# Summing squares on VectorE in fp32 ahead of the ones-matmul of every norm

## The chip, the cores and the metric

The kernel runs on all 8 cores of one Trainium2 chip. Each core has one sequence of the batch and the cores exchange nothing. The metric is the device time in microseconds (us) of the slowest core. A program on 8 cores has a second, slower state in some of its executions: the cores of one die, or of both, show a lower granted TensorE clock, and the run is longer. Only fast runs are compared here, unless a sentence says otherwise.

The notes on the chip that this document draws on are called the Trainium skill; its pages are named by their titles.

## The reference, cut to what matters

A decoder block: a SwiGLU feed-forward (FFN1), a token mixer (a convolution branch beside a linear recurrence), a second SwiGLU feed-forward (FFN2), a final norm. Sequence 4096, width 1024, hidden width 2816. Every stage starts with a root-mean-square norm, and the convolution branch has a layer norm over 512 channels.

```python
def rmsnorm(x, g):
    xf = x.astype(jnp.float32)
    y = xf * lax.rsqrt(jnp.mean(xf * xf, axis=-1, keepdims=True) + EPS)
    return y.astype(x.dtype) * g

def layernorm(x, g, b):
    xf = x.astype(jnp.float32)
    mu = jnp.mean(xf, axis=-1, keepdims=True)
    var = jnp.mean(jnp.square(xf - mu), axis=-1, keepdims=True)
    ...

def swiglu_ffn(h, w_in, w_out):
    gate, up = jnp.split(h @ w_in, 2, axis=-1)
    return (jax.nn.silu(gate) * up) @ w_out
```

## The kernel before

Channels lie on partitions and tokens on the free axis. A tile is 512 tokens; its 1024 channels are 8 chunks of 128 x 512 in fp32. So a mean over channels is a sum over the 8 chunks and over the 128 partitions. The kernel does both on TensorE: each chunk is squared into a bf16 buffer, and a matmul with a 128 x 128 matrix of ones, accumulated in PSUM over the chunks, leaves the total on every partition.

```python
def stats(xs, after=(), prio=None):
    bank = new(ps, "st")
    for f in range(8):
        q = new(p1, "xsq")                        # a bf16 buffer
        o, i = (lambda q=q: q.ap), (lambda f=f: xs[f].ap)
        act(o, i, AF.Square, [xs[f]], [q], after=after, prio=prio, alt=v_sq(o, i))
        mms(bank, [(k_(ones.ap), lambda q=q: q.ap)], [q, ones], first=(f == 0), last=(f == 7), prio=prio)
    r = new(p2, "r")                              # then 1/sqrt as exp(-0.5 ln(.)) on ScalarE
    ...
```

`alt` lets a list scheduler put the square on VectorE instead of ScalarE. There are four such statistics per tile (FFN1, mixer, FFN2, final), so 32 of 8 ones-matmuls. The layer norm sums 4 chunks and their squares, 8 ones-matmuls in each of 8 tiles:

```python
bm, bq = new(ps, "lm"), new(ps, "lq")
for c in range(4):
    b, q = new(p1, "cvb"), new(p1, "cvsq")
    cp(lambda b=b: b.ap, lambda c=c: cv[c].ap, [cv[c]], [b])      # cast to bf16 on VectorE
    act(o, i, AF.Square, [cv[c]], [q], alt=v_sq(o, i))
    mms(bm, [(k_(ones.ap), lambda b=b: b.ap)], [b, ones], first=(c == 0), last=(c == 3))
    mms(bq, [(k_(ones.ap), lambda q=q: q.ap)], [q, ones], first=(c == 0), last=(c == 3))
```

That is 32 x 8 + 8 x 8 = 320 ones-matmuls.

The scheduler orders every instruction of the program ahead of time. Among the operations that can start now on an engine it takes the lowest `prio`, else the one that can start first, with planned durations. Each engine, the DMA-issuing ones (SP, POOL) included, then works through its own list in order, with semaphore waits:

```python
now = s <= et[e] + 0.03
key = (0 if now else 1, op.prio + (sw and 0.5) if now else s + sw, op.idx)
```

Three more places matter. FFN1 runs first for all tiles, in pairs, with `prio` 500 to 800, and stores its result x to DRAM ("xmid"). Then mixer, FFN2 and final norm run tile by tile, and read xmid back:

```python
def mix_ffn2(t):
    P.prio = 1000 + 10 * t
    gate_op = (last_in, anchors[-1][1])[t] if t < 2 else ffn_anchor[t - 2]
    xs = load_x(xm_dr, t, after=(gate_op,) * 8)     # 8 loads of 256 KB, issued by SP
    hb = norm(xs, M_SC2, M_SH2, prio=940)           # the mixer norm
```

Weights come in "slabs" of 128 x 2048 bf16 through ten slab buffers. On first use a slab is cast on its way in by a POOL DMA, and written back to DRAM in bf16 by SP for later tiles. Most weights of the second phase are cast during FFN1 (`prep`), but not those of FFN2's down-projection, "w2o", whose 12 slabs are cast on first use, in tile 0:

```python
def load_slab(nm, r, cast, prio=None, after=()):
    b = new(sl, f"{nm}{r}")
    if cast:
        dma("PL", lambda: b.ap, lambda: src, D_CAST, ..., [], [b], slab=True, ...)   # fp32 -> bf16
        dma("SP", lambda: d.ap, lambda: b.ap, D_SLAB, ..., [b], [d], prio=prio)      # write back
    else:
        dma("SP", lambda: b.ap, lambda: d.ap, D_SLAB, slot_sem(b), [d], [b], slab=True, ...)
...
prep = [(nm, r) for nm in ("win", "dcw", "wout", "w2i") for r in range(len(scr[nm]))]
...
slabs = [load_slab("w2o", 3 * q + s, t == 0) for s in range(3)]
```

## Time and profile before

| | before |
|---|---|
| device time, 3 fast runs | 2488.01, 2489.81, 2493.35 us |
| spans of the cores in the profiled run | 2468.5 to 2483.8 us, granted clock 0.991 to 0.993 |
| ones-matmuls | 320 |
| one more matmul in a dense row | 0.216 us |
| one fp32 128x512 VectorE add | 0.683 us |

The page of the slowest core, core 6: span, busy time by engine, TensorE's busy tenths in 40 slices of the span, and the shares of the chain that ended last (followed back from the last instruction, at each step to what released it). PEld is TensorE's loading of weights; a q after a name is the queue that waits and issues for that engine.

```profile
span 2483.8 us, 34258 instructions; the slowest of 8 cores (2468.5 to 2483.8 us)
PE 2361.1 (95%) x11177; PEld 1114.5 (45%) x11392; DVE 1057.8 (43%) x1795; ACT 911.9 (37%) x1382; POOL 115.2 (5%) x221
PE   1999999999999999899899999999999999999996
PE 90%; DMA 5%; ACT 2%; issue 1%; SPq 1%; DVE 1%; POOL 0%; DVEq 0%; POOLq 0%; ACTq 0%
```

TensorE (PE) is the bound: 95% busy, 90% of the chain. The four slices that aren't 9 are where it stands still: the start (weights arrive by DMA), slices 17 and 20 (the first mixer norm, and a stop near 1230 us) and the tail. VectorE (DVE) has more than half of its time free.

Groups of instructions of the same core, shapes kept apart. The columns after the count are busy us and mean ns of one; then the idle time of the engine before them and what ended most of it.

```profile
L443 PE MATMUL ps<-sb_h,sb_ones 128*128 128x512 bf16 x313 | 106.6, 394 | 67.0 <-ACT sb_h L401 59.6 <-DVE sb_h L413 6.5
L443 PEld LDWEIGHTS ps<-sb_h,sb_ones 128*128 128x128 bf16 x320 | 31.2, 98 | 118.5 <-issue 92.6
L423 DVE TENSOR_TENSOR sb_c<-sb_c 128x512 f32<-128x512 f32 x96 | 61.6, 683 | 11.1 <-ACT sb_c L401 11.0
L433 DVE CAST sb_h<-sb_c 128x512 bf16<-128x512 f32 x64 | 25.9, 420 | 0.6
```

The trace has lost 7 of the 320 ones-matmuls, but none of their weight loads, so weight loads are what to count by. A mean of 394 ns isn't what one costs: matmuls are pipelined, and their ends are modelled. The cost is read from starts. The timeline of PE in the steady part, core 6, columns start, us, instruction:

```profile
1334.16 0.38 PE L443 MATMUL ps<-sb_h,sb_ones 128*128 128x512 bf16 x1
1334.37 1.89 PE L443 MATMUL ps<-sb_h,sb_slab 128*128 128x512 bf16 x8
1336.10 0.38 PE L443 MATMUL ps<-sb_h,sb_ones 128*128 128x512 bf16 x1
```

The ones-matmul starts at 1334.16 and the next matmul at 1334.37: 0.21 us, no more than between any two of the eight that follow (1336.10 - 1334.37 = 1.73 us for 8). So 224 ones-matmuls are worth at most 224 x 0.216 = 48 us.

The stop near 1230 us is the second place to know. PE on core 6, then the issue queue of SP, then the chain of waits over the same stretch:

```profile
1214.70 12.47 PE L443 MATMUL ps<-sb_h,sb_slab 128*128 128x512 bf16 x56
1236.60 0.58 PE L443 MATMUL ps<-sb_h,sb_ones 128*128 128x512 bf16 x1 [9.43 <-ACT sb_h L401]
1236.98 6.18 PE L443 MATMUL ps<-sb_h,sb_slab 128*128 128x512 bf16 x16
```

```profile
1193.31 29.86 SPq L450 DMA_DIRECT2D b_w2o<-sb_slab  x7
1223.37 4.96 SPq L450 DMA_DIRECT2D sb_c<-xmid  x8
```

```profile
1207.86 14.94 DMA sb_slab<-w2o
...
1223.37 12.38 DMA sb_c<-xmid
...
1235.83 0.64 ACT sb_h L401
```

PE stands 9.43 us before the ones-matmul at 1236.60. The profile names ScalarE (ACT), but its square took 0.64 us: the chain shows that it waited for an xmid load, issued at 1223.37 and landed 12.38 us later, and that SP could issue it only after a writeback that itself waited for a cast of w2o, which took 14.94 us from issue to landing. The stop costs a second time. The windows view gives the busy time of PE, PEld, DVE, ACT and POOL in a stretch, the granted clock, the DMA share and GB/s:

```profile
1227.00:1237.00 10.00, 0.57 (x3) 0.23 (x3) 1.44 (x2) 1.15 (x2) 0.00 (x0) 0.75 1.05 251
1237.00:1243.00 6.00, 6.00 (x18) 2.17 (x17) 0.00 (x0) 3.15 (x5) 0.00 (x0) 0.57 0.97 305
1500.00:1680.00 180.00, 178.14 (x875) 86.55 (x890) 91.31 (x159) 89.53 (x134) 4.31 (x8) 1.00 0.55 182
```

The Trainium skill, "TensorE: Matmul & The Clock Gate", section "What's actually happening", says that an idle window of about 3.4 us halves the clock and a busy one of that length restores it. The trace agrees: the granted clock after the stop is 0.57, and 16 matmuls take 6.18 us where a warm row would take 15 x 0.216 + 0.38 = 3.62. In the single records the first thirteen start 0.43 us apart and the last three 0.21 to 0.25: the full rate is back about 5.5 us after the stop ends. The DMA engines are full at 1.05 during the stop. The last line is the steady part: PE busy 178.14 of 180 us, VectorE 91.31.

### The profile page before, as it was taken

What the parts mean: (1) busy time and instruction counts of PE and PEld (TensorE: products, weight loads), DVE (VectorE), ACT (ScalarE), POOL (GpSimd) and SP (SyncE); (2) the same over time, 40 slices, a digit from 0 to 9 for tenths busy, and PEclk for the clock granted to TensorE, in tenths of its full rate; (3) what the DMA queues carried; (4) which work ended last, traced back from release to release, by engine and by line L of the source; (5) the groups of instructions that cost most, each with busy time, mean ns of one, the idle gap of its engine ahead of it and who ended that gap; (6) DMA issues with size and microseconds to landing.
All of it is one profiled execution on the core that took longest, in us unless ns stands there. A gap on an engine that the chain in (4) does not pass through costs nothing.

```text
span 2483.8 us, 34258 instructions; the slowest of 8 cores (2468.5 to 2483.8 us)
## 1 busy us (share of the span) xinstructions
PE 2361.1 (95%) x11177; PEld 1114.5 (45%) x11392; DVE 1057.8 (43%) x1795; ACT 911.9 (37%) x1382; POOL 115.2 (5%) x221
## 2 busy tenths in 40 slices
PE   1999999999999999899899999999999999999996
PEld 0444444444444444454354454454454454454442
DVE  3413133423342332785166175184274274373121
ACT  3213011301131120676157265265364364364122
POOL 0100100010001001000000000000000000000000
PEclk9999999999999999899999999999999999999998
DMA  9899489669856764554966555555555545555451
GB/s 274 192 217 230 160 213 221 165 189 220 221 166 181 188 189 164 163 166 159 200 207 203 186 179 178 187 178 179 187 178 178 187 170 187 187 170 186 153 188 66
DMA packets 131708, 460.31 MB, mean 185 GB/s; under 512 B 16048, under 2 KB 16176, under 8 KB 130864
## 3 DMA queue, kind: packets, MB, share of 16 engines
q1 hardware_dynamic: 113184, 378.15, 47.0%
q0 software_dynamic: 18352, 79.97, 16.0%
q8 instruction: 96, 1.57, 0.3%
q14 instruction: 76, 0.62, 0.1%
HBM read 446.78 MB, written 79.69 MB: 212 GB/s over the span
## 4 chain that ended last, share of the span: by engine, by line
PE 90%; DMA 5%; ACT 2%; issue 1%; SPq 1%; DVE 1%; POOL 0%; DVEq 0%; POOLq 0%; ACTq 0%
PE ps L443 90%; DMA sb_slab<-wmod 2%; DMA sb_c<-x 1%; SPq L450 1%; DMA sb_c<-xmid 1%; ACT sb_c L401 1%; DMA sb_slab<-w2o 1%; ACT sb_h L401 1%; DVE sb_c L419 0%; DVE sb_c L409 0%; DVE sb_slab L499 0%; DVE sb_ub L419 0%; ACT L401 0%; POOL y L450 0%; DVEq L113 0%
## 5 line engine op out<-in xcount | busy, mean ns | idle before, releaser
L443 PE MATMUL ps<-sb_h,sb_slab 128*128 128x512 bf16 x9776 | 2182.2, 380 | 28.7 <-ACT sb_h L401 15.8
L443 PEld LDWEIGHTS ps<-sb_h,sb_slab 128*128 128x128 bf16 x9984 | 977.7, 98 | 1196.1 <-issue 30.4
L423 DVE TENSOR_TENSOR sb_h<-ps,sb_c 128x512 bf16<-128x512 f32 x352 | 241.7, 691 | 784.0 <-PE ps L443 706.5
L401 ACT ACTIVATE sb_c<-ps 128x512 f32<-128x512 f32 x400 | 237.2, 596 | 882.0 <-PE ps L443 858.5
L401 ACT ACTIVATE sb_h<-sb_c 128x512 bf16<-128x512 f32 x241 | 148.9, 628 | 387.2 <-DVE sb_c L419 234.4
L419 DVE SCALAR_TENSOR_TENSOR sb_c<-ps,sb_gth,sb_c 128x512 f32<-128x512 f32 x128 | 95.2, 749 | 399.1 <-PE ps L443 390.6
L401 ACT ACT_TABLE_LOAD x102 | 130.9, 1283 | 211.5 <-PE ps L443 199.2
L419 DVE SCALAR_TENSOR_TENSOR sb_c<-sb_c,sb_gs 128x512 f32<-128x512 f32 x256 | 173.6, 745 | 39.9 <-ACT sb_c L401 39.9
L443 PE MATMUL ps<-sb_h,sb_ones 128*128 128x512 bf16 x313 | 106.6, 394 | 67.0 <-ACT sb_h L401 59.6
L499 DVE SCALAR_TENSOR_TENSOR sb_slab<-sb_slab,sb_crow 128x1024 f32<-128x1024 f32 x88 | 107.0, 1217 | 34.1 <-DMA sb_slab<-wmod 33.6
L443 PE MATMUL ps<-sb_ub,sb_slab 128*128 128x256 bf16 x1024 | 115.0, 273 | 4.3 <-DVE sb_c L409 3.3
L401 ACT ACTIVATE sb_h<-sb_c,sb_modv 128x512 bf16<-128x512 f32 x162 | 107.4, 719 | 15.6 <-DVE sb_modv L423 8.8
L443 PEld LDWEIGHTS ps<-sb_ub,sb_slab 128*128 128x128 bf16 x1024 | 99.5, 98 | 21.5 <-issue 8.1
L450 POOL DMA_DIRECT2D y<-sb_c x64 | 34.5, 540 | 1144.6 <-ACT sb_c L401 1104.7
L443 PEld LDWEIGHTS ps<-sb_h,sb_ones 128*128 128x128 bf16 x320 | 31.2, 98 | 118.5 <-issue 92.6
L419 DVE SCALAR_TENSOR_TENSOR sb_c<-ps,sb_modv,sb_c 128x512 f32<-128x512 f32 x64 | 48.0, 750 | 72.7 <-PE ps L443 72.5
L419 DVE SCALAR_TENSOR_TENSOR sb_c<-sb_ux,sb_vecs,sb_c 128x512 f32<-128x512 f32 x96 | 69.2, 743 | 1.3
L423 DVE TENSOR_TENSOR sb_c<-sb_c 128x512 f32<-128x512 f32 x96 | 61.6, 683 | 11.1 <-ACT sb_c L401 11.0
L419 DVE SCALAR_TENSOR_TENSOR sb_ub<-sb_c,ps 64x256 bf16<-64x256 f32 x128 | 53.8, 420 | 15.3 <-PE ps L443 11.8
L401 ACT ACTIVATE sb_c<-sb_c,sb_lam 128x512 f32<-128x512 f32 x64 | 49.1, 824 | 0.2
L450 POOL DMA_DIRECT2D xmid<-sb_c x64 | 34.8, 544 | 295.6 <-DVE sb_c L419 280.6
L401 ACT ACTIVATE sb_c<-sb_c 128x512 f32<-128x512 f32 x72 | 44.0, 626 | 2.2
(51 smaller groups left out, 532.8 us busy)
## 6 DMA issues: line engine op xcount, KB each, us to landing
sb_slab<-b_w2i SPq DMA_DIRECT2D x176, 512.0 KB, 3.8
sb_slab<-wmod SPq DMA_DIRECT2D x88, 512.0 KB, 6.1
sb_slab<-b_w2o SPq DMA_DIRECT2D x84, 512.0 KB, 3.7
sb_slab<-b_w1i SPq DMA_DIRECT2D x66, 512.0 KB, 6.0
sb_slab<-b_win SPq DMA_DIRECT2D x64, 512.0 KB, 4.0
sb_slab<-b_dcw SPq DMA_DIRECT2D x64, 512.0 KB, 3.6
sb_slab<-b_w1o SPq DMA_DIRECT2D x36, 512.0 KB, 5.5
sb_c<-x SPq DMA_DIRECT2D x64, 256.0 KB, 11.0
```

The lines of the kernel that those rows point to most:

```text
L401: return A("ACT", dur, lambda: (lambda o, i: (lambda h: [h.activation(out=o, in_=i, func=func, bias=bias, scale=scale)]))(out(), in_()), r ...
L419: return A("DVE", dur, lambda: (lambda o, a, b: (lambda h: [h.scalar_tensor_tensor(out=o, in0=a, scalar=scalar, in1=b, op0=op0, op1=op1)]) ...
L423: return A("DVE", dur, lambda: (lambda o, a, b: (lambda h: [h.tensor_tensor(out=o, in0=a, in1=b, op=op)]))(out(), in0(), in1()), reads, wr ...
L443: return [h.matmul(o, lhsT=l, rhs=r, start=(first and i == 0), stop=(last and i == n - 1)) for i, (l, r) in enumerate(pr)]
L450: lambda: (lambda o, i: (lambda h: [h.dma_start(out=o, in_=i)]))(out(), in_()),
L499: return lambda h: [h.scalar_tensor_tensor(out=w, in0=w, scalar=1.0, in1=crow.ap, op0=ALU.mult, op1=ALU.mult, accum_out=o)]
```

## The change

The intent: add the fp32 squares of four chunks on VectorE, which has time, and give TensorE the sum, so that a statistic needs 2 ones-matmuls instead of 8. In the layer norm, chunks and squares are added in pairs: 4 ones-matmuls instead of 8, and the pair add writes bf16, so it replaces two casts. The squares move from bf16 to fp32 buffers. The first hunk, which only gives the helper `tt` a `prio` argument, is cut.

```diff
# (the hunk of the helper tt is cut)
@@ -532,11 +532,19 @@
         def stats(xs, after=(), prio=None):
 
             bank = new(ps, "st")
-            for f in range(8):
-                q = new(p1, "xsq")
-                o, i = (lambda q=q: q.ap), (lambda f=f: xs[f].ap)
-                act(o, i, AF.Square, [xs[f]], [q], after=after, prio=prio, alt=v_sq(o, i))
-                mms(bank, [(k_(ones.ap), lambda q=q: q.ap)], [q, ones], first=(f == 0), last=(f == 7), prio=prio)
+            for hf in range(2):
+                acc, sm = None, None
+                for f in range(4 * hf, 4 * hf + 4):
+                    q = new(p2, "xsq")
+                    o, i = (lambda q=q: q.ap), (lambda f=f: xs[f].ap)
+                    act(o, i, AF.Square, [xs[f]], [q], after=after, prio=prio, alt=v_sq(o, i))
+                    if acc is None:
+                        acc = q
+                        continue
+                    d = acc if f % 4 < 3 else new(p1, "sqb")
+                    tt(lambda d=d: d.ap, lambda q=q: q.ap, lambda acc=acc: acc.ap, ALU.add, [q, acc], [d], prio=prio)
+                    acc = d
+                mms(bank, [(k_(ones.ap), lambda d=acc: d.ap)], [acc, ones], first=(hf == 0), last=(hf == 1), prio=prio)
             r = new(p2, "r")
             act(lambda: r.ap, lambda: bank.ap, AF.Ln, [bank, cst], [r], bias=eps_ap, scale=1.0 / D, tset=(NLE,), prio=prio)
             act(lambda: r.ap, lambda: r.ap, AF.Exp, [r], [r], scale=-0.5, tset=(NLE,), prio=prio)
@@ -745,13 +753,20 @@
             A("DVE", 0.25, lambda: (lambda h: [h.tensor_copy(out=ub_t[:, :, 0:15], in_=ub_t[:, :, 256:271])]), [], ub)
 
             bm, bq = new(ps, "lm"), new(ps, "lq")
-            for c in range(4):
-                b, q = new(p1, "cvb"), new(p1, "cvsq")
-                cp(lambda b=b: b.ap, lambda c=c: cv[c].ap, [cv[c]], [b])
-                o, i = (lambda q=q: q.ap), (lambda c=c: cv[c].ap)
-                act(o, i, AF.Square, [cv[c]], [q], alt=v_sq(o, i))
-                mms(bm, [(k_(ones.ap), lambda b=b: b.ap)], [b, ones], first=(c == 0), last=(c == 3))
-                mms(bq, [(k_(ones.ap), lambda q=q: q.ap)], [q, ones], first=(c == 0), last=(c == 3))
+            for c in range(2):
+                a, e = cv[2 * c], cv[2 * c + 1]
+                b = new(p1, "cvb")
+                tt(lambda b=b: b.ap, lambda a=a: a.ap, lambda e=e: e.ap, ALU.add, [a, e], [b])
+                sq = []
+                for v in (a, e):
+                    q = new(p2, "cvsq")
+                    o, i = (lambda q=q: q.ap), (lambda v=v: v.ap)
+                    act(o, i, AF.Square, [v], [q], alt=v_sq(o, i))
+                    sq.append(q)
+                q = new(p1, "cvsb")
+                tt(lambda q=q: q.ap, lambda s=sq[0]: s.ap, lambda s=sq[1]: s.ap, ALU.add, sq, [q])
+                mms(bm, [(k_(ones.ap), lambda b=b: b.ap)], [b, ones], first=(c == 0), last=(c == 1))
+                mms(bq, [(k_(ones.ap), lambda q=q: q.ap)], [q, ones], first=(c == 0), last=(c == 1))
             mean, var = new(p2, "mean"), new(p2, "var")
             act(lambda: mean.ap, lambda bm=bm: bm.ap, AF.Copy, [bm], [mean], scale=1.0 / 512)
             act(lambda: var.ap, lambda bm=bm: bm.ap, AF.Square, [bm], [var], scale=1.0 / 512)
```

> **What bounds the kernel.** TensorE. The page gives PE 2361 of 2484 us busy (95%); the chain of waits is 90% PE; VectorE is at 43%, ScalarE at 37%. Matmuls start every 0.216 us (chain pieces of 10.74 us hold 49). The Trainium skill, "TensorE: Matmul & The Clock Gate", section "Wait — 56ns, not 53.3ns?", has 215.7 ns for a warm 512-column bf16 matmul; the trace agrees. In 180 us of the steady part PE is busy 178.3 (windows view). PE stands still in four places: before 65.8 us (weights by DMA), 5 us before 232 (a late x chunk ahead of a ones-matmul), about 11 us in 1000-1012 (first mixer norm), 9.4 us before 1236.6 (late xmid).
>
> **Removed.** 32 root-mean-square statistics go from 8 ones-matmuls to 2, and 8 layer norms from 8 to 4: 320 ones-matmuls become 96, 224 fewer. A lone one pushes the next matmul back by 0.22 us in the timeline (1334.16 to 1334.37), so weight switching adds nothing. At most 224 x 0.216 = 48 us (1.9%).
>
> **What does not count.** 12 of the first pair run while PE waits for weights; 12 of the second pair stand in the wait that ends at 232; 12 of the first mixer norms in the stop at 1000-1012; the last tile's 6 in the wait for the last square. Left: 182 x 0.216 = 39 us.
>
> **Added.** 192 fp32 adds, and 32 pair adds for 32 casts, on VectorE: 192 x 0.69 + 32 x (0.69 - 0.42) = about 141 us, to about 1200 us (49%). That two-input fp32 form lasts 0.683 us in the trace. The Trainium skill, "VectorE: DVE Perf Modes", section on mode 2x_2P, says fp32 tensor_tensor stays at 1x; the trace agrees, beside 0.42 for the one-input cast. Per steady tile that is 18 adds, 12.4 us, on 91.5 of 180 us. VectorE is 80-98% busy for only some 40 us around the recurrence and the convolution's evictions; there I expect 0.4 us more PE waiting per tile, about 3 us. Each statistic ends one add later (0.8 us), bare only in the tail and at one or two stage starts: 1.5 us. The squares move to the 40-buffer fp32 pool; the order listing shows later x loads displaced by only one or two places, so I charge nothing.
>
> **Reordering.** In the PE order the second pair's ones-matmuls now come after 16 to 28 more weight matmuls, and at the mixer's start two instead of sixteen precede the first projection matmuls. The stops at 227-232 and 1000-1012 may shrink by 0-4 us each: about 3 us together.
>
> **Sum.** 2490 - 39 - 3 + 3 + 1.5 = about 2452 us, 1.5% faster; range 2443 to 2463. Faster by over 2% (under 2440) needs nearly all 48 us or a stop to vanish: 7%. Within 2%: 92%. Slower: 1%.
>
> **What would show it.** Ones-matmuls x96; PE busy down 45-50 us by the page; the steady tile's period down from 179.5 to about 175 us; 240-990 shorter by about 5 us (24 fewer matmuls); VectorE near 1200 us; the tail 0.8 us longer; PE's waits for VectorE adds a few us in all.
>
> **What would make it wrong.** An add waiting for a late x or xmid chunk, in VectorE's in-order queue ahead of SwiGLU products or evictions, stalls PE (a longer stop at 220-236 or 1227-1240); more PE waiting in the mixer from VectorE; the fp32 pool running short and delaying loads; the stops at stage starts shifting by more than 4 us.

## The result, and the profile after

| | before | after |
|---|---|---|
| fast runs of the same rounds | 2488.01, 2489.81, 2493.35 us | 2449.68, 2452.52, 2454.54 us |
| slow runs | 2537.59 us | 2525.91 us (one die at clock 0.957 to 0.969) |
| ratio of fast runs, 95% interval | | 0.9847 (0.9823 to 0.987) |

Ratios are computed as the mean time of one kernel's fast runs over that of the other's in the same rounds, so not quite the ratio of the medians. The change makes the kernel 1.5% faster, within 2%. The median of its fast runs, 2452.52 us, is 0.5 us from the predicted 2452; over all four runs, the slow one included, it is 2453.53. In later rounds the same kernel ran 2441.01 to 2443.34 us, ratio 0.983 to the kernel before of those rounds. The outcome agrees; the question of the experiments is whether the sum agrees for the reasons given.

The page of the slowest core after, core 7, the same four parts:

```profile
span 2451.0 us, 34505 instructions; the slowest of 8 cores (2429.1 to 2451.0 us)
PE 2322.6 (95%) x11168; PEld 1094.5 (45%) x11168; DVE 1177.5 (48%) x1968; ACT 920.1 (38%) x1400; POOL 115.8 (5%) x221
PE   0999999999999999799999999999999999999996
PE 82%; DMA 7%; SPq 4%; ACT 2%; issue 2%; DVE 2%; POOL 0%; ACTq 0%; DVEq 0%; POOLq 0%
```

TensorE is still the bound. VectorE's busy time rose by 119.7 us and cost TensorE a few us. The prediction had added 141 us: it missed that the scheduler moved squares to ScalarE (VectorE does 47 of 288 before and 25 after). In the slices, the dip near 1230 us (slice 20) is gone, but the one of the first mixer norm (slice 17) is deeper, 7 instead of 8. The groups after, core 7:

```profile
L443 PE MATMUL ps<-sb_h,sb_ones 128*128 128x512 bf16 x96 | 34.7, 396 | 68.7 <-DVE sb_h L423 68.5
L423 DVE TENSOR_TENSOR sb_c<-sb_c 128x512 f32<-128x512 f32 x224 | 149.1, 687 | 85.4 <-ACT sb_c L401 83.6 <-DVE sb_c L413 0.2
L423 DVE TENSOR_TENSOR sb_h<-sb_c 128x512 bf16<-128x512 f32 x96 | 65.1, 689 | 22.4 <-ACT sb_c L401 20.0
L433 DVE CAST sb_h<-sb_c 128x512 bf16<-128x512 f32 x32 | 13.5, 422 | 0.2
```

96 ones-matmuls, 224 fewer. The idle time before them is about the same in sum (67.0 and 68.7 us), and the add now comes last where the square did. Most of it is at the program's start (40 us before, 47 after); but in the steady part core 7 now waits once per tile, 0.7 to 2.3 us, for an add. An add lasts 687 to 689 ns, close to the 683 of before. Steady part, core 7, the windows view:

```profile
1655.00:1830.00 175.00, 173.45 (x865) 84.25 (x864) 103.40 (x176) 90.12 (x134) 4.30 (x8) 1.00 0.58 187
```

VectorE went from 91 to 103 us per tile, and PE is still busy all but 1.6 us (3.2 us in the window 1500 to 1675 of the same core). The place of the stop, core 6: PE, then SP's issue queue.

```profile
1184.81 33.40 PE L443 MATMUL ps<-sb_h,sb_slab 128*128 128x512 bf16 x151
1221.25 0.58 PE L443 MATMUL ps<-sb_h,sb_ones 128*128 128x512 bf16 x1 [3.04 <-DVE sb_h L423]
1221.63 2.75 PE L443 MATMUL ps<-sb_h,sb_slab 128*128 128x512 bf16 x6
1225.89 0.38 PE L443 MATMUL ps<-sb_h,sb_ones 128*128 128x512 bf16 x1 [1.50 <-DVE sb_h L423]
```

```profile
1180.52 19.19 SPq L450 DMA_DIRECT2D b_w2o<-sb_slab  x5
1199.86 0.55 SPq L450 DMA_DIRECT2D sb_slab<-b_win  x1
1203.71 0.32 SPq L450 DMA_DIRECT2D b_w2o<-sb_slab  x1
1204.19 0.78 SPq L450 DMA_DIRECT2D sb_slab<-b_win  x1
1209.09 0.32 SPq L450 DMA_DIRECT2D b_w2o<-sb_slab  x1
1209.60 4.54 SPq L450 DMA_DIRECT2D sb_c<-xmid  x8
```

The stop of 9.43 us has become two of 3.04 and 1.50 us. In both kernels seven writebacks stand ahead of the eight xmid loads, so the loads didn't move ahead of any; two slab loads (b_win) now stand ahead of them besides. But between the issue of the first load and the moment PE runs out of work there were 1227.17 - 1223.37 = 3.8 us before and there are 1218.21 - 1209.60 = 8.6 us after (1227.17 and 1218.21 are the ends of PE's row in the timelines). The prediction has no term for that. The casts, issued by POOL, are the other difference; before, then after, core 6:

```profile
1211.31 0.53 POOL L450 DMA_DIRECT2D sb_slab<-w2o  x1 [2.92 <-PE ps L443]
1214.76 0.53 POOL L450 DMA_DIRECT2D sb_slab<-w2o  x1 [2.93 <-PE ps L443]
1218.21 0.53 POOL L450 DMA_DIRECT2D sb_slab<-w2o  x1 [2.93 <-PE ps L443]
```

```profile
1195.44 0.53 POOL L450 DMA_DIRECT2D sb_slab<-w2o  x1 [2.91 <-PE ps L443]
1218.75 0.53 POOL L450 DMA_DIRECT2D sb_slab<-w2o  x1 [22.78 <-PE ps L443]
```

Before, these three are in flight when the first xmid load is issued at 1223.37. After, no cast is issued for 23 us around the load at 1209.60.

To see where the time went I cut the trace into stretches bounded by equal amounts of weight-matmul work, counted at 0.216 us for 512 columns and 0.108 for 256. Idle is duration, minus work, minus 0.216 us for each ones-matmul. All are medians of the 8 cores, so they don't add up exactly to the median span.

| stretch (us of weight work done) | before: duration, ones, idle | after: duration, ones, idle | difference in duration |
|---|---|---|---|
| start, to the first weight matmul | 65.6, 16, 62.1 | 66.9, 4, 66.0 | +1.3 |
| 0 to 200: holds the second pair's norm | 210.4, 16, 7.0 | 208.2, 4, 7.4 | -2.2 |
| 300 to 900: the third and fourth pair | 606.5, 32, -0.4 | 601.3, 8, -0.4 | -5.2 |
| 900 to 1000: the first mixer norm | 124.9, 32, 18.0 | 123.7, 10, 21.5 | -1.2 |
| 1000 to 1130: holds the stop near 1230 us | 147.9, 24, 12.7 | 138.2, 8, 6.5 | -9.7 |
| 1130 to 1330 | 209.0, 32, 2.1 | 205.2, 10, 3.0 | -3.8 |
| 1330 to 2180: five steady tiles | 891.6, 160, 7.1 | 870.7, 50, 10.1 | -20.9 |
| tail, after the last weight matmul | 22.9, 8, 20.9 | 23.8, 2, 23.2 | +0.9 |

Stretches of pure weight matmuls that are the same in both are left out. The sum is -40.8 us; the median of the cores' spans fell from 2478.2 to 2440.4 us. The cleanest row is 300 to 900: 24 ones-matmuls fewer, 5.2 us shorter, which is 24 x 0.216 to the tenth.

### The profile page after: what moved, and what is told of

It reads as the page before. It is cut to its first block, busy times and chain, and to the rows that moved or that the text cites. A ratio compares the mean times of both kernels' runs of the same rounds, so it can differ in the third digit from the quotient of the medians.

```text
span 2451.0 us, 34505 instructions; the slowest of 8 cores (2429.1 to 2451.0 us)
## 1 busy us (share of the span) xinstructions
PE 2322.6 (95%) x11168; PEld 1094.5 (45%) x11168; DVE 1177.5 (48%) x1968; ACT 920.1 (38%) x1400; POOL 115.8 (5%) x221
## 4 chain that ended last, share of the span: by engine, by line
PE 82%; DMA 7%; SPq 4%; ACT 2%; issue 2%; DVE 2%; POOL 0%; ACTq 0%; DVEq 0%; POOLq 0%
PE ps L443 82%; SPq L450 4%; DMA sb_c<-xmid 2%; DMA sb_slab<-w1i 2%; ACT sb_c L401 2%; DMA sb_c<-x 1%; DMA sb_slab<-wmod 1%; DMA sb_slab<-w2o 1%; DMA b_w1i<-sb_slab 1%; DVE sb_c L732 0%; DVE sb_c L409 0%; DVE sb_h L423 0%; ACT L401 0%; ACT sb_h L401 0%; DVE sb_c L423 0%
## 5 line engine op out<-in xcount | busy, mean ns | idle before, releaser
L401 ACT ACTIVATE sb_c<-sb_c 128x512 f32<-128x512 f32 x335 | 205.8, 627 | 346.6 <-DVE sb_c L419 188.1
L423 DVE TENSOR_TENSOR sb_c<-sb_c 128x512 f32<-128x512 f32 x224 | 149.1, 687 | 85.4 <-ACT sb_c L401 83.6
L401 ACT ACTIVATE sb_h<-sb_c,sb_modv 128x512 bf16<-128x512 f32 x162 | 105.6, 715 | 18.3 <-DVE sb_modv L423 10.1
L443 PE MATMUL ps<-sb_h,sb_ones 128*128 128x512 bf16 x96 | 34.7, 396 | 68.7 <-DVE sb_h L423 68.5
L423 DVE TENSOR_TENSOR sb_h<-sb_c 128x512 bf16<-128x512 f32 x96 | 65.1, 689 | 22.4 <-ACT sb_c L401 20.0
L443 PEld LDWEIGHTS ps<-sb_h,sb_ones 128*128 128x128 bf16 x96 | 9.2, 99 | 86.4 <-issue 79.5
```

The lines of the kernel that those rows point to most:

```text
L401: return A("ACT", dur, lambda: (lambda o, i: (lambda h: [h.activation(out=o, in_=i, func=func, bias=bias, scale=scale)]))(out(), in_()), r ...
L423: return A("DVE", dur, lambda: (lambda o, a, b: (lambda h: [h.tensor_tensor(out=o, in0=a, in1=b, op=op)]))(out(), in0(), in1()), reads, wr ...
L443: return [h.matmul(o, lhsT=l, rhs=r, start=(first and i == 0), stop=(last and i == n - 1)) for i, (l, r) in enumerate(pr)]
```

## The experiments

Twelve kernels ran, all with correct results. The first eight below ran on one chip (four, then four in later rounds), the next three on a second, the last on a third; each is compared with the kernel before of its own rounds, and across chips by that ratio. The means below are of fast runs. The texts on record were written before each run.

### The removed slots, given back

The theory: the gain is TensorE's slots. A rival: it is the reordering, or the loads. The changed kernel gets 224 matmuls with a matrix of zeros, so the count is 320 again with the results unchanged.

```diff
+zer = fixed("zer", [128, 128], BF16)          # memset to 0.0
-mms(bank, [(k_(ones.ap), ...)], [acc, ones], ...)
+mms(bank, [(k_(ones.ap), ...)] + [(k_(zer.ap), ...)] * 3, [acc, ones, zer], ...)
 # and one zero matmul beside each ones-matmul of the layer norm
```

> The changed kernel with the 224 removed matmuls put back as matmuls by an all-zero weight tile on the same summed squares (right result, 320 matmuls again, the adds stay). Theory (TensorE slots pay): the gain goes; 182 to 212 of the 224 stand outside stops, so 39 to 46 us more than the change: 2490 to 2502 us, with idle as in the change. Rival (the gain comes from the new order of instructions and shorter stops at stage starts, with freed slots refilled by waits): under 2470 us.

Measured: 2478.65 to 2482.35 us, mean 2480.14, ratio 0.9986 (0.9968 to 1.0003). The changed kernel on the same chip, in later rounds, has a mean of 2442.44, so the slots are worth 37.7 us, just under the expected range. The rival falls. A zero matmul takes the slot of a ones-matmul: the stretch 300 to 900 is back at 606.5 us. A gain of 3.5 us over the kernel before (2483.6, from the ratio) is left with all slots given back, but the interval reaches 1, so it isn't clear of noise. The trace does show the shorter stop: the stretch 1000 to 1130 has 5.4 us of idle, against 12.7 before.

### Each half alone

Only the root-mean-square statistics are changed; the layer norm is as before.

```diff
-for c in range(2):   # pair adds of the layer norm
+for c in range(4):   # cast, square and two ones-matmuls per chunk, as before
```

> Only the root-mean-square statistics summed by fours; layer norm as before. 192 matmuls fewer. Theory: the layer norm's 32 matmuls are worth 32 x 0.216 = 6.9 us less about 1 us of waits, so this is 5 to 7 us slower than the whole change: 2458 to 2462 us. Rival (the layer norm part, where VectorE is fullest, costs more than it saves): equal to the whole change or faster, 2448 to 2454 us.

Measured: 2449.28 to 2452.54 us, mean 2450.54 (one slow run of 2849.08), ratio 0.9869 (0.9845 to 0.9893). That is 8.1 us slower than the whole change of the later rounds on the same chip, a little over the expected range.

Only the layer norm is changed; `stats` is as before.

> Only the layer norm in pairs; statistics as before. 32 matmuls fewer, all in the steady flow. Theory: 5 to 7 us faster than before, 2484 to 2487 us, plus or minus up to 6 us if the stop near 1230 us moves. Rival (VectorE there is full, waits eat it): same as before, 2490 to 2494 us.

Measured: 2475.93 to 2481.14 us, mean 2478.26 (one slow run), ratio 0.9978 (0.9958 to 0.9998), a gain of 5.4 us. 32 ones-matmuls less are 32 x 0.216 = 6.9. Its idle in 1000 to 1130 stays at 11.2 us, and in the kernel with the statistics alone it is 6.5: the statistics shrink the stop, not the layer norm.

### Doubled adds

If VectorE's adds cost PE time, twice as many should cost it again. Each add gets a dummy one beside it, 192 in all.

```diff
 tt(... ALU.add, [q, acc], [d], prio=prio)
 acc = d
+jk = new(p2, "jk")
+tt(lambda jk=jk: jk.ap, lambda f=f: xs[f].ap, lambda f=f: xs[f].ap, ALU.add, [xs[f]], [jk], prio=prio)
```

> The change with every added add of the statistics doubled by one whose result nobody reads: 192 more fp32 two-input operations, about 132 us more VectorE work. Theory (VectorE has room; the measured extra idle of 0.6 us per steady tile came with the first 192): 3 to 8 us slower than the change, 2456 to 2462 us. Rival (VectorE nearly bounds the mixer, adds are paid in full there): 6 adds per statistic in the fullest stretch, over 15 us slower, above 2469 us.

Measured: 2459.70 and 2459.89 us undisturbed; a run of 2482.39 counted as fast has two cores at clock 0.979 and 0.978, and one of 2498.62 is slow. So about 17 us over the changed kernel of the later rounds (2442.44): the time is inside the theory's range in absolute terms, the difference inside the rival's, so the totals decide nothing. Where the time went does, and it is what neither expected. In the steady part the doubled adds cost nothing: on the four undisturbed cores the idle of five tiles is 2.0, 2.4, 1.5, 2.1 and 1.0 us, against 2.8, 2.2, 1.9, 2.2 and 1.0 in the table's kernel. Nearly all of the cost is at the beginning: against the repeated change, the first weight matmul comes 5.9 us later and the stretch 0 to 200 takes 9.0 us more (medians of 8 cores). Core 2, VectorE and then PE:

```profile
174.14 0.69 DVE L423 TENSOR_TENSOR sb_c<-sb_c 128x512 f32<-128x512 f32 x1 [19.00 <-DMA sb_c<-x]
174.75 0.68 DVE L423 TENSOR_TENSOR sb_h<-ps,sb_c 128x512 bf16<-128x512 f32 x1
```

```profile
154.69 13.98 PE L443 MATMUL ps<-sb_h,sb_slab 128*128 128x512 bf16 x64
175.58 6.77 PE L443 MATMUL ps<-sb_h,sb_slab 128*128 128x512 bf16 x23 [6.91 <-DVE sb_h L423]
```

A dummy add stands 19.00 us in VectorE's queue for a late chunk of x. Behind it stands a SwiGLU product that PE needs, and PE stops for 6.91 us. The Trainium skill, "TensorE: Matmul & The Clock Gate", the specification table at its top, calls VectorE's queue a strict FIFO; these lines agree. It is partly an artefact of mine: the dummy adds lack the gate that holds the squares of later tiles back, so the scheduler planned them too early. The real adds follow their squares and are gated with them.

### The stop near 1230 us taken away, from both kernels

If the shorter stop is luck of order and no part of the change's worth, taking it away on both sides should leave the pure trade. The w2o weights are cast during FFN1 like the others, so no cast and no writeback is left beside the xmid loads.

```diff
-prep = [(nm, r) for nm in ("win", "dcw", "wout", "w2i") for r in ...]
+prep = [(nm, r) for nm in ("win", "dcw", "wout", "w2i", "w2o") for r in ...]
-slabs = [load_slab("w2o", 3 * q + s, t == 0) for s in range(3)]
+slabs = [load_slab("w2o", 3 * q + s, False) for s in range(3)]
```

The changed kernel, repeated beside them for the comparison:

> The changed kernel again, as the yardstick on this chip for the three others of this call: ratio to before 0.982 to 0.987.

Measured: 2441.01 to 2443.34 us, mean 2442.44, ratio 0.983 (0.9815 to 0.9844). The kernel before has 2484.7 by that ratio.

The kernel before with w2o prepared:

> The kernel before, with the second down projection's weights (w2o) cast to bf16 in the prepared list during the first phase, so that no cast and no writeback of them stands in the queues when the third tile's xmid chunks are loaded. Theory (the stop of about 12 us near 1227-1240 is the xmid loads waiting behind six w2o writebacks in SP's in-order queue): the stop goes to under 3 us, 7 to 11 us faster than before. Rival (xmid is late because the memory channels are full there): the stop stays at 9 us or more, time within 3 us of before.

Measured: 2469.47, 2470.70 and 2472.57 us (four more runs were slow, over 2764 us), mean 2470.91, ratio 0.9944 (0.9928 to 0.9961). The gain of 13.8 us is more than expected. The idle in 1000 to 1130 fell from 12.7 to 0.4 us. The expected cause, six writebacks ahead in SP's queue, isn't singled out: the edit takes the casts away too. PE on core 6 at that place:

```profile
1200.00 18.94 PE L443 MATMUL ps<-sb_h,sb_slab 128*128 128x512 bf16 x86
1218.78 0.38 PE L443 MATMUL ps<-sb_h,sb_ones 128*128 128x512 bf16 x1
1218.99 1.46 PE L443 MATMUL ps<-sb_h,sb_slab 128*128 128x512 bf16 x6
```

No wait stands before the ones-matmul. The changed kernel with w2o prepared:

> The change with the same preparation of w2o. Theory (6 us of the change's gain were the xmid loads moving ahead of four writebacks in SP's order, by accident): 3 to 6 us faster than the change, and only 32 to 35 us faster than before with w2o prepared. Rival (the shorter stop comes from the fewer matmuls themselves): still 37 us or more between the two prepared kernels.

Measured: 2435.65 to 2437.93 us, mean 2436.86 (three slow runs), ratio 0.9807 (0.9793 to 0.9822). The prepared kernels differ by 2470.91 - 2436.86 = 34.1 us, where the unprepared ones of the same rounds differ by 2484.7 - 2442.44 = 42.3. So about 8 us of the change's gain on this chip were a shorter stop and not the trade itself; the trade is worth 34 us, 1.4%. (From the scatter of these runs I estimate plus or minus 3 us on the 8 and 2 on the 34.) Both numbers expected came out, 5.6 us under the change and 34.1 between the prepared kernels, but the reason on record didn't: no xmid load moved ahead of a writeback.

Why did the stop shrink? Medians of the 8 cores, for the third tile's xmid loads, from the trace (times count from the issue of the first of the eight):

| | first load lands | PE's row of matmuls ends | in flight at that issue: w2o casts, writebacks, slab loads |
|---|---|---|---|
| before | 13.8 us | 4.6 us | 3, 3, 0 |
| after | 6.4 us | 8.6 us | 0, 2, 2 |
| layer norm alone | 13.8 us | 5.0 us | 3, 3, 0 |
| statistics alone | 6.6 us | 8.7 us | 0, 2, 2 |
| change, zeros put back | 6.1 us | 7.8 us | 0, 2, 2 |
| before, w2o prepared | 4.7 us | 6.3 us | 0, 0, 2 |
| after, w2o prepared | 4.6 us | 8.4 us | 0, 0, 1 |

Two things moved. The planner let two projection slabs (b_win in the issue queue) take slab buffers ahead of the next casts, so seven casts instead of ten had been issued by then and none was in flight when the first xmid load was issued, which landed in half the time. That the casts made the difference is read from these rows; no run varied them alone. And PE's first ones-matmul of that tile now waits for four squares and stands 3.4 us of weight matmuls later in PE's list. Both come with the statistics part, with or without the slots.

### One ones-matmul per statistic

If an add costs nothing in the steady part, sum all 8 chunks on VectorE.

```diff
-for hf in range(2):
+for hf in range(1):
-    for f in range(4 * hf, 4 * hf + 4):
+    for f in range(8 * hf, 8 * hf + 8):
```

> All eight squares summed ahead of a single ones-matmul per statistic: 32 matmuls fewer than the change. Theory (TensorE slots pay, an add costs nothing in the steady flow): 22 to 28 of the 32 stand in the steady flow, 3 to 6 us faster than the change, idle per steady tile unchanged within 0.5 us. Rival (later statistics make TensorE wait): same as the change or slower, idle per steady tile up by 1 us or more.

Measured: 2435.35 to 2437.88 us, mean 2436.04 (one slow run), ratio 0.9802 (0.9787 to 0.9817): 6.4 us faster than the changed kernel. 32 slots are 6.9 us, so the 32 more adds cost nothing that shows; the idle of the five steady tiles even fell, from 10.3 us in the repeated change to 7.2.

### Both together, and two tries at the ends

One ones-matmul per statistic and w2o prepared:

> Both gains together: all eight squares summed ahead of one ones-matmul, and w2o prepared early. Theory (the two act in different stretches and add up): 4 to 8 us faster than either alone, ratio to before 0.977 to 0.979. Rival (the later single sums meet other late loads): no faster than the better of the two, 0.980 or more.

Measured: 2430.06 to 2435.93 us, mean 2432.64, ratio 0.979 (0.9776 to 0.9804). The ratio is at the edge of the expected range, but the two gains don't add: by ratio it is 0.0012, or 3 us, ahead of the summed kernel alone, under the 4 to 8 expected, and the two intervals overlap.

What is left of idle is the first mixer norm: 25.2 us in the stretch 900 to 1000. The theory for the next one was that the second tile's norm gets in the way of the first's, so it is put later.

```diff
-hb = norm(xs, M_SC2, M_SH2, prio=940)
+hb = norm(xs, M_SC2, M_SH2, prio=1005 if t == 1 else 940)
```

> e9 with the second tile's first mixer norm at a lower priority than the first tile's matmuls, so that its ones-matmul no longer stands in TensorE's queue ahead of them while its xmid chunks land. Theory (the idle of 22 to 25 us around 1000 us is partly that ones-matmul at the head of the queue): idle there falls by 3 to 10 us, the time by as much against e9. Rival (it is the load and the first tile's own norm that take so long): idle there within 2 us of e9.

Measured: 2429.86 to 2435.42 us, mean 2432.30, ratio 0.9791: no gain, and the theory falls. The stretches 900 to 1130 take 261.9 us together, against 260.8. The idle moved to a second stop of 9.64 us at 1050 us, in front of the second tile's own work.

With it, the statistics at the program's start and the last tile's final norm go back to 8 ones-matmuls (`flat`), since there the slots are free and the adds stand bare.

```diff
-hbs = [norm(xs, M_SC1, M_SH1, after=(last_in,), prio=300) for xs in xss]
+hbs = [norm(xs, M_SC1, M_SH1, after=(last_in,), prio=300, flat=pi == 0) for xs in xss]
-r = stats(xs)
+r = stats(xs, flat=t == n_tiles - 1)
```

> e10 with the statistics left unsummed, eight ones-matmuls each, where TensorE stands still anyway: the first pair's first norms and the last tile's final norm. Theory (a sum there only makes the chain longer by one add): tail 0.7 to 1.0 us shorter, first weight matmul 0 to 1.5 us earlier, 1 to 2 us faster than e10. Rival (nothing there is bare): within 0.5 us of e10 in both places.

Measured: 2430.63 to 2432.37 us, mean 2431.73 (two slow runs), ratio 0.9786 (0.9772 to 0.98). The tail is 0.8 us shorter (22.3 against 23.1), the start unchanged (66.1 both). In the total it can't be told from noise.

### The first tile's norm, earlier

The other theory for that stop: FFN1's last matmuls have `prio` 800, so the first tile's norm at 940 is left until they have run out, though its data is there. Earlier means a lower number, with the kernel of one ones-matmul and prepared w2o as the base.

```diff
-hb = norm(xs, M_SC2, M_SH2, prio=940)
+hb = norm(xs, M_SC2, M_SH2, prio=700 if t == 0 else 940)
```

> e9 with only the first tile's first mixer norm raised above the last FFN1 matmuls in priority, so that its ones-matmul, table load, logarithm, exponential and eight products run while TensorE still has those matmuls. Theory (the stop of 13 us before the first mixer matmul is this norm's own chain, left until FFN1's matmuls are through): idle in the stretch around it falls from 25 to under 17 us and the time by 7 to 12 us against e9, to 0.974 to 0.976 of before. Rival (the second tile's late xmid chunks, ahead in the in-order queues, hold it): idle within 4 us of e9.

Measured: 2413.55 to 2418.22 us (one slow run), ratio 0.972 (0.9704 to 0.9737). This is the best kernel, 2.8% faster than the one before and about 17 us faster than its base by the ratios (0.007 of 2485), more than expected. The idle of 900 to 1000 fell from 25.2 to 6.2 us; 1000 to 1130 took 3.9 us back. PE on core 6 at that place in the base, then here:

```profile
982.25 0.38 PE L443 MATMUL ps<-sb_h,sb_ones 128*128 128x512 bf16 x1
995.63 2.72 PE L443 MATMUL ps<-sb_h,sb_slab 128*128 128x512 bf16 x6 [13.00 <-ACT sb_h L401]
```

```profile
913.26 0.38 PE L443 MATMUL ps<-sb_h,sb_ones 128*128 128x512 bf16 x1
913.48 78.73 PE L443 MATMUL ps<-sb_h,sb_slab 128*128 128x512 bf16 x364
```

In the base the ones-matmul came last and the rest of the norm followed it with nothing for PE to do. Here it runs at 913.26, and 364 recorded weight matmuls cover the rest.

## Why the prediction was right, and where it wasn't

The prediction, 2452 us, was right: the change is worth TensorE's slots at 0.216 us each, less those that stood in a wait anyway, and VectorE's adds cost only a few us. Point by point:

- **TensorE's slots: right.** The row 300 to 900 gives 5.2 us for 24 matmuls, and putting the slots back costs 37.7 us. Over all stretches but start and tail, 206 ones-matmuls went, 44.5 us.
- **VectorE: right.** 1177.5 us busy, predicted about 1200. Idle per steady tile rose by (10.1 - 7.1) / 5 = 0.6 us, predicted 0.4; with the slots given back and the adds kept it is 9.1, so 0.4. On the slowest core of the profiled run, core 7, it rose by 1.9 us (6.5 to 16.0 in five tiles), which the repeated run doesn't show (8.9). Doubling the adds raised nothing there.
- **Steady part: right.** A stretch of 170 us of work takes 870.7 / 5 = 174.1 us instead of 178.3.
- **PE busy time: nearly right.** Predicted down by 45 to 50 us by the page, it shows 38.5, but the two pages are of different cores: core 6 of the page before lacks 2% of its matmul records (11177 of 11392, against the weight loads), core 7 of the page after none (11168 of 11168). Cores 0 and 6 lack records in both kernels. Core 6 against core 6 it fell from 2361.1 to 2307.9 us; on the six complete cores the median fell from 2371.3 to 2320 us. So it is 51 to 53 us.
- **The tail: right.** +0.9 us, predicted 0.8. The start, +1.3, was in the same term.
- **"The stops at 227-232 and 1000-1012 may shrink by 0-4 us each: about 3 us together": mis-sized.** The second pair's stretch became 2.2 us shorter, and 6.9 us in the repeated run (the stretch there against that of the first trace before). The first mixer norm didn't shrink: its idle rose from 18.0 to 21.5 us, so 12 of its removed slots and 3.5 - 12 x 0.216 = about 1 us more turned into waiting. The last experiment shows why fewer ones-matmuls can't help there: the first tile's own norm was left until the last weight matmul of FFN1 had gone.
- **"later x loads displaced by only one or two places, so I charge nothing": the term that was missing.** I had looked at the x loads and named the stop near 1230 us only as one that might grow. Its stretch lost 6.2 us of idle (12.7 to 6.5). No writeback had left its place ahead of the xmid loads; what moved was which casts run beside them and how much work PE has left.

The two errors have opposite signs and partly cancelled. The sum of the table shows it: 44.5 us of slots, less 3.5 lost again at the first mixer norm, less 3.0 in the steady part, 0.4 and 0.9 in two others and 2.2 at the ends, plus 6.2 from the stop, leaves 40.7, against 40.8 in the table. The prediction's own terms come to 38. The device time of the first comparison, 38.1 us between the means of the fast runs (2490.4 and 2452.2), hits that figure with a gain in it that nobody had foreseen: that it fits to the microsecond is luck. With the stop gone from both kernels the change is worth 34 us, and in the later rounds with the stop it was worth 42; both are inside the predicted range (27 to 47 us), so the verdict doesn't hang on the luck.

What stays open: which part of the cast matters to the xmid loads, its reads, its writes or the writeback, since the experiment took them away together; and which core is the slowest, which changes from run to run without a cause that these runs show (core 5 had a span of 2429.9 us in one fast run of the changed kernel and of 2453.0 in the next).

## What to carry to other kernels

A matmul that only adds along chunks costs its full slot wherever TensorE is dense and nothing wherever it waits, so count the slots by stretch before trading them for adds on an idle engine. An add is free there only if nothing that TensorE needs stands behind it in the same queue while it waits for late data. When a static scheduler decides the order, read the DMA queues after the change too: here the largest surprise, and the best kernel, came from when loads and one norm ran, not from the work removed.

## What the Trainium skill lacked or had wrong

- "TensorE: Matmul & The Clock Gate", section "Seeing it yourself", says that three or more cores of a die with dense matmuls take the die to 13/16 of the clock, and to budget 1.95 GHz for all-core work on the default power profile. Here 8 cores run dense bf16 matmuls, and in fast runs the mean granted clock is 0.989 to 0.997 on every core (0.978 and 0.979 on two cores of one run with doubled adds), with 0.216 us per matmul. Only slow runs show lower clocks: one die at 0.957 to 0.969 (2525.91 us), or at 0.828 to 0.829 (2857.69 us). The last is near 13/16 = 0.81, but no run here shows what causes it, and the power profile isn't on record.
- "DMA: Bandwidth & Descriptors", section "Issuing engines are not separate DMA queues", says that DMAs of all issuers interleave on the same 16 engines. These runs fit that, and add the size that the page lacks: of eight 256 KB loads the first landed after 13.8 us with three casts of another issuer and three writebacks in flight, after 6.4 us with no cast, two writebacks and two 512 KB loads, and after 4.7 us with two such loads alone.
- No page that I read says what a wait inside an in-order issue queue costs the transfers behind it: eight loads stood behind a writeback that waited for a 14.94 us cast, and PE stopped for 9.43 us.
